# Scan of a bidirectional Mamba-2 branch: its decay matrices formed by TensorE in PSUM instead of by ScalarE, VectorE and GpSimd from broadcast rows

## The chip, the cores and the metric

The program runs on one core of a Trainium2 chip. The metric is the device time of one execution in microseconds (us), the median of several runs. The engines are named as the profile names them: PE is TensorE, DVE is VectorE, ACT is ScalarE, POOL is GpSimd and SP is SyncE, whose queue issues all the DMAs here.

## What is computed

The kernel is one layer of a diffusion backbone: a normalised input of 1024 tokens by 1024 channels feeds three branches (a bidirectional state-space scan, a Fourier mixing and a gated MLP), their outputs are gated and merged, and a feed-forward part with a short convolution follows. The change touches the scan alone. Its reference, cut to that part, for one direction:

```python
cum = jnp.cumsum(dt * a, axis=-1)                      # per chunk of 128 tokens, per head
lmat = jnp.exp(jnp.where(tri_q, cum[..., :, None] - cum[..., None, :], -jnp.inf))
cb = jnp.einsum('bcqgn,bcsgn->bcgqs', cf, bf)
y_diag = jnp.einsum('bcgqs,bgrcqs,bcsgrp->bcqgrp', cb, lmat, xf)   # xf = x * dt
y_off = jnp.einsum('bcqgn,bcgrpn,bgrcq->bcqgrp', cf, prev, jnp.exp(cum))
y = y_diag + y_off
```

The second direction runs over the flipped sequence with its own `dt` and `a`, and the two results are added. There are 16 heads of 64 channels in two groups of 8, and 8 chunks of 128 tokens. For each chunk and head a matrix of 128 by 128 factors is needed: the forward one below the diagonal plus the backward one above it, each exp of a difference of two running sums times a step size, times `cb`, which all heads of a group share.

## The kernel before, in words

The products with the big weight matrices run over all 1024 tokens. Each output tile of 128 channels is 48 products of 128 by 128 weights with 512 columns (`mm3`, L145 to L157: weights and inputs are split in a high and a low fp32r part, three products for each of 8 blocks and 2 halves). Its result lies in a PSUM tile of 1024 columns from the pool `psm` (tag `mm`, two buffers, `ps_big`, L48). The other four PSUM banks are single buffers with the tags `c`, `c2`, `t` and `y` (`ps_small`). PSUM is then full.

The scan of one group is `ssd_group`. It is called for group 0 after the context tokens' states are known (`ctx_state`), and for group 1 after `group_in(1)`, which computes group 1's inputs: tiles 9 and 11 (the `B` and `C` of the scan), x tiles 4 to 7, and, as filler between them, the tiles of the Fourier branch (`f_tile`, `psf0` to `psf3`). Behind the second scan stand the tiles `psz0` to `psz3`, `psu0` to `psu3` and `psv0`, `psv1`. A scheduler orders the instructions of each engine at build time, by priority and by what its own model takes to be free; it may put products of a later big tile between those of the scan, as far as their PSUM buffer is free. The engines then run their queues strictly in that order.

In one chunk `c` of `ssd_group` the steps are these. `y_off` (L511 to L519) runs once for the forward and once for the backward direction: two DMAs broadcast a chunk's running sums from DRAM into a tile `ro` (`decay_rows`, tag `ro` with two buffers, of which each direction in effect has one), ACT takes exp of it (L504), PE forms `po` from the state `st` (L514), DVE multiplies the two (L517) and POOL or DVE adds the result to `yacc` (L519). `state_step` (L521 to L531) carries the state on: POOL scales X and the old state, PE forms `pS` (L527), DVE adds (L531). Between them, for two half groups of four heads (`hg`): two DMAs of 256 KB broadcast the running sums of both directions (`rload`, L495: tiles `rf` and `rs`). For each head ACT subtracts the column's sum (L561), DVE subtracts the other direction's and takes the smaller of the two (L562), ACT and DVE form from the two masked copies of `cb` a matrix `G` of step sizes times `cb` (L564, L565). ACT takes exp of four heads at once (L567), POOL multiplies with `G` (L568), PE multiplies with X into `py` (L573), and DVE adds `py` to `yacc` (L576).

The lines that steer this:

```python
psm = pool("psm", bufs=2, space=bass.MemoryType.PSUM)
...
def ps_big(name):
    return psm.tile([P, 1024], F32, tag="mm", name=name)
...
r = s3.tile([P, 4, P], F32, tag="ro", name=f"ro{d_}{g}{c}")
```

Of the kernel before, what the change touches and what calls it, by code (L numbers as in the profile page):

```python
# [32 lines left out]
def hybrid_block_kernel(ctx: ExitStack, tc: tile.TileContext, a, dbg=None):  # L33
# [18 lines left out]
    def ps_small(name, tag="c"):  # L52
        return pss.tile([P, 512], F32, tag=tag, name=name)
# [6 lines left out]
    def bc(ap, shape):  # L60
        return ap.broadcast_to(shape)
# [430 lines left out]
    def rload(c, d_, g, hg, nm, tag):  # L492
        r = s3.tile([P, 4, P], F32, tag=tag, name=f"{nm}{g}{c}{hg}")
        o = d_ * 16 + g * 8 + hg * 4
        SY.dma_start(r, Rd[c, o:o + 4, :].partition_broadcast(P))  # L495
        return r
# [37 lines left out]
    def xload(g, c, nm):  # L534
        X = s3.tile([P, 512], F32, tag="X" + nm, name=f"X{nm}{g}{c}", bufs=2 if nm == "f" else 1)
        SY.dma_start(X, Xd[g][c])
        return X

    def ssd_group(g, BT, Bt, CT):
# [6 lines left out]
        scr[1, g] = s3.tile([P, L], F32, tag="scr", name=f"scr1{g}", bufs=1)  # L546
        for c in range(NCH):
            X = xload(g, c, "f")
            pcb = ps_small(f"pcb{g}{c}", "c")
            PE.matmul(pcb[:, 0:P], BT[:, c * P:(c + 1) * P], CT[:, c * P:(c + 1) * P], start=True, stop=True)  # L550
            cbm = s3.tile([P, 2, P], F32, tag="cbm", name=f"cbm{g}{c}", bufs=1)
            V.tensor_tensor(cbm, bc(pcb[:, 0:P].unsqueeze(1), [P, 2, P]), msk, op=ALU.mult)  # L552
            y_off(g, c, 0, stf, CT, G)
            py = ps_small(f"py{g}{c}", "y")
            for hg in range(2):
                E = rload(c, 0, g, hg, "rf", "rf")
                rs = rload(c, 1, g, hg, "rs", "rs")
                Gm = s3.tile([P, 4, P], F32, tag="G", name=f"G{g}{c}{hg}")
                for h in range(4):
                    f = g * 8 + hg * 4 + h  # L560
                    S.activation(E[:, h, :], E[:, h, :], AF.Identity, bias=ncum[:, c, f:f + 1])  # L561
                    V.scalar_tensor_tensor(E[:, h, :], rs[:, h, :], ncum[:, c, 16 + f:17 + f], E[:, h, :],  # L562
                                           op0=ALU.add, op1=ALU.min)
                    S.activation(Gm[:, h, :], cbm[:, 0, :], AF.Copy, scale=dtl[:, c, f:f + 1])  # L564
                    V.scalar_tensor_tensor(Gm[:, h, :], cbm[:, 1, :], dtl[:, c, 16 + f:17 + f], Gm[:, h, :],  # L565
                                           op0=ALU.mult, op1=ALU.add)
                S.activation(E, E, AF.Exp)  # L567
                G.tensor_tensor(E, E, Gm, op=ALU.mult)  # L568
                for h in range(4):
                    hd = (4 * hg + h) * 64  # L570
                    j = h % 2
                    i = 2 * hg + h // 2
                    PE.matmul(py[64 * j:64 * j + 64, i * P:(i + 1) * P], X[:, hd:hd + 64], E[:, h, :],  # L573
                              start=True, stop=True)
# [24 lines left out]
    Rd = dram.tile([NCH, 32, P], F32, name="Rd")  # L599
    psr = ps_small("psr")  # L600
    for i in range(2):
        PE.transpose(out=psr[:, i * P:(i + 1) * P], in_=cums[:, 4 * i:4 * i + 4, :].rearrange("p c h -> p (c h)"),
                     identity=ident)
    Rs_ = ddp.tile([P, 2, P], F32, tag="ul", name="Rs_")
    S.activation(Rs_, psr[:, 0:2 * P].rearrange("p (i q) -> p i q", i=2), AF.Copy)
    SY.dma_start(Rd.rearrange("(i c) h q -> (c h) i q", i=2), Rs_)
    yacc[0] = mpool.tile([P, 4, L], F32, tag="m", name="yacc0")
# [10 lines left out]
    s3 = pool("s3", bufs=2, side="right")  # L618
    ssd_group(0, *gi)
# [1064 lines left out]
def prepare(i):  # L1684
# [9 lines left out]
    r["tabc"], r["tabl"] = tabc, tabl  # L1694
    wm = i["w_mod"][0]
# [49 lines left out]
```

## Time and profile before

| what | value |
|---|---|
| runs shown (three) | 1888.46, 1881.87, 1887.11 us; median 1887.11 |
| the profiled execution | 1883.76 us, its span 1882.0 us |
| PE busy / weight loads | 1747.4 us (93%) / 1409.2 us (75%) |
| DVE, ACT, POOL busy | 1383.9 us (74%), 859.9 us (46%), 856.0 us (45%) |
| granted TensorE clock, mean | 0.967 |
| DMA | 268.75 MB, mean 143 GB/s |

The span is the part of the execution in which the engines ran instructions; 1.8 us lie around it. Busy shares count the time between an instruction's start and its (for PE modelled) end, so that a PE shown as busy may still stream fewer columns than it could: its records overlap. Where a stage is to be judged, the start of one product to the start of the next tells more than the busy share.

### The profile page before, as it was taken

How to read it: one execution, taken by the hardware profiler on the slowest of the kernel's cores; microseconds unless marked ns; L12 is line 12 of the kernel's file. 1: busy time of each engine (PE TensorE's matmuls, PEld its weight loads, DVE VectorE, ACT ScalarE, POOL GpSimd, SP SyncE). 2: the span in 40 equal slices, each digit the busy share in tenths (PEclk: the TensorE clock that was granted, in tenths of full speed). 3: DMA queues.
4: the chain of work that ended last, by engine and by line, in shares of the span. 5: the costliest groups of instructions: out<-in, count | busy, mean ns of one | idle time of the engine just before them, and what ended most of it. 6: DMA issues, size and time to landing. Idle time of an engine off the chain costs nothing. (4 is left out here: it accounts for less than half of the span.)

```text
span 1882.0 us, 23647 instructions
## 1 busy us (share of the span) xinstructions
PE 1747.4 (93%) x8148; PEld 1409.2 (75%) x8148; DVE 1383.9 (74%) x1983; ACT 859.9 (46%) x1480; POOL 856.0 (45%) x579
## 2 busy tenths in 40 slices
PE   4899998988989989999899999799999999899988
PEld 2688776766668868888688888578888888677777
DVE  7875577777573675557949536998888889967896
ACT  6644355564442344444524234445555455533433
POOL 3322355556531464554645745633333333544553
PEclk9999999999999989999998999899999999999998
DMA  9211365553454225765346464122232225553532
GB/s 336 101 59 61 118 191 159 154 159 116 148 183 160 107 85 184 235 224 184 118 146 201 129 230 140 40 90 96 95 126 104 96 96 174 199 187 106 174 111 90
DMA packets 148064, 268.75 MB, mean 143 GB/s; under 512 B 15836, under 2 KB 56668, under 8 KB 146536
## 3 DMA queue, kind: packets, MB, share of 16 engines
q1 hardware_dynamic: 147944, 267.25, 43.0%
q8 instruction: 64, 1.05, 0.2%
q14 instruction: 56, 0.46, 0.1%
HBM read 209.90 MB, written 57.29 MB: 142 GB/s over the span
## 5 line engine op out<-in xcount | busy, mean ns | idle before, releaser
L293 DVE SCALAR_TENSOR_TENSOR acc<-psx,convw,acc 128x1023 f32<-128x1023 f32 (+1 forms) x48 | 61.3, 1277 | 22.5 <-ACT acc L289 22.1
L562 DVE SCALAR_TENSOR_TENSOR rf<-rs,ncuml,rf 128x128 f32<-128x128 f32 x128 | 52.2, 454 | 32.4 <-ACT rf L561 29.2
L1272 POOL TENSOR_TENSOR pwo<-rwo,pwo 128x512 fp32r<-128x512 f32 x32 | 46.8, 1467 | 48.5 <-ACT pwo L1271 43.4
L857 POOL TENSOR_TENSOR w1up<-A11up,w1up 128x512 fp32r<-128x512 f32 x20 | 26.8, 1342 | 89.8 <-ACT w1up L856 80.6
L568 POOL TENSOR_TENSOR rf<-rf,G 128x512 f32<-128x512 f32 x32 | 46.1, 1442 | 43.1 <-DVE G L565 33.0
L857 POOL TENSOR_TENSOR w7up<-S3up,w7up 128x512 fp32r<-128x512 f32 x20 | 28.8, 1438 | 77.5 <-ACT w7up L856 45.0
L565 DVE SCALAR_TENSOR_TENSOR G<-cbm,dtl,G 128x128 f32<-128x128 f32 x128 | 57.0, 504 | 5.1 <-ACT G L564 5.1
L1561 DVE SCALAR_TENSOR_TENSOR xf<-Yd,g,xf 128x512 f32<-128x512 f32 x64 | 47.1, 743 | 13.0 <-PE Yd L867 12.7
L561 ACT ACTIVATE rf<-rf,ncuml 128x128 f32<-128x128 f32 x128 | 41.1, 389 | 29.5 <-DMA rf<-Rd 29.3
L166 ACT ACTIVATE gh<-gr 128x1024 fp32r<-128x1024 f32 (+1 forms) x36 | 37.1, 1034 | 38.0 <-DMA gr<-Gd 37.1
L157 PE MATMUL pso<-mh,pwo 128*128 128x512 f32 x128 | 50.2, 392 | 0.0
L153 PE MATMUL pso<-mh,pwo 128*128 128x512 f32 x128 | 49.8, 390 | 0.0
L155 PE MATMUL pso<-ml,pwo 128*128 128x512 f32 x128 | 49.8, 389 | 0.0
L517 DVE TENSOR_TENSOR scr<-po,ro 128x512 f32<-128x512 f32 x32 | 21.8, 683 | 35.2 <-ACT ro L504 35.0
L527 PE MATMUL pS<-scr,Bt 128*128 128x512 f32 x56 | 32.9, 671 | 15.4 <-DVE scr L517 12.0
L504 ACT ACTIVATE ro<-ro 128x512 f32<-128x512 f32 x32 | 20.1, 627 | 57.4 <-DMA ro<-Rd 57.1
L564 ACT ACTIVATE G<-cbm,dtl 128x128 f32<-128x128 f32 x128 | 39.6, 388 | 7.4 <-DVE cbm L552 7.4
L167 DVE TENSOR_TENSOR gl<-gr,gh 128x1024 fp32r<-128x1024 f32 (+1 forms) x26 | 39.7, 1527 | 4.2 <-ACT gh L166 3.6
L1477 DVE TENSOR_TENSOR gt<-gt,aa 128x512 f32<-128x512 f32 x44 | 42.5, 967 | 0.1
L1474 ACT ACTIVATE ft<-aa 128x512 f32<-128x512 f32 x44 | 27.8, 631 | 30.0 <-DVE aa L1456 29.0
L529 POOL TENSOR_TENSOR st<-st,etl 128x512 f32<-128x512 f32 x24 | 26.5, 1106 | 31.6 <-DVE st L531 31.6
L857 POOL TENSOR_TENSOR w4up<-A22up,w4up 128x512 fp32r<-128x512 f32 x20 | 30.9, 1544 | 21.4 <-ACT w4up L856 21.4
(1291 smaller groups left out, 6622.6 us busy)
## 6 DMA issues: line engine op xcount, KB each, us to landing
gr<-Gd SPq DMA_DIRECT2D x70, 256.0 KB, 3.7
Gd<-gt SPq DMA_DIRECT2D x10, 1536.0 KB, 5.7
wm<-in_wmod_dram SPq DMA_DIRECT2D x16, 512.0 KB, 9.6
ro<-Rd SPq DMA_DIRECT2D x64, 128.0 KB, 3.3
rf<-Rd SPq DMA_DIRECT2D x32, 256.0 KB, 4.3
rs<-Rd SPq DMA_DIRECT2D x32, 256.0 KB, 3.8
ctanh<-in_wmod_dram SPq DMA_DIRECT2D x32, 256.0 KB, 4.3
crow<-in_wmod_dram SPq DMA_DIRECT2D x32, 256.0 KB, 4.4
```

Of the source, the lines that this page charges most:

```text
L153: PE.matmul(o, wh[:, k, :], xh[:, sl], start=st, stop=False)
L155: PE.matmul(o, wh[:, k, :], xl[:, sl], start=False, stop=False)
L157: last_op["mm"] = PE.matmul(o, wl[:, k, :], xh[:, sl], start=False, stop=sp)
L293: V.scalar_tensor_tensor(acc[:, lo:hi], ps[:, lo + o:hi + o], cw[:, t, j:j + 1], acc[:, lo:hi], op0=ALU.mult, op1=ALU.add)
L561: S.activation(E[:, h, :], E[:, h, :], AF.Identity, bias=ncum[:, c, f:f + 1])
L562: V.scalar_tensor_tensor(E[:, h, :], rs[:, h, :], ncum[:, c, 16 + f:17 + f], E[:, h, :], op0=ALU.add, op1=ALU.min)
L565: V.scalar_tensor_tensor(Gm[:, h, :], cbm[:, 1, :], dtl[:, c, 16 + f:17 + f], Gm[:, h, :], op0=ALU.mult, op1=ALU.add)
L568: G.tensor_tensor(E, E, Gm, op=ALU.mult)
L857: (V if p in on_v else G).tensor_tensor(t[:, 1, :], ap, f32(t)[:, 0, :], op=ALU.subtract)
L1272: G.tensor_tensor(t[:, 1, :], raw, f32(t)[:, 0, :], op=ALU.subtract)
L1477: V.tensor_tensor(gt[:, 2 * q + h, :], gt[:, 2 * q + h, :], aa[:, HS[h]], op=ALU.mult)
L1561: V.scalar_tensor_tensor(xv, src, g2[:, dd:dd + 1], xv, op0=ALU.mult, op1=ALU.add)
```

## The change

Per chunk, half group and direction, the exponents of four heads come from TensorE. Each running sum is split into two fp32r parts, high and low, and written to DRAM as rows (`Rr[0]`); a second set of rows holds the logarithm of the step size less the running sum (`Rr[1]`, from a Ln on ACT, which brings two loads of activation tables). Before a scan, `Lt` is filled with ones and with the rows of the second set; for each chunk and direction two rows of the first set are loaded into `Rt`, under 16 rows of zeros and ones. A product of 18 rows, `Lt` with `Rt`, gives the 128 by 512 exponents, and a second product of the identity with `neg` adds -1e30 where the mask excludes (L498, L499). Both directions' exponents stand in one PSUM tile `E` of `ps_big`, the pool of the big tiles. ACT takes exp of each half (L575, L576), DVE adds the halves (L577) and multiplies with `cb` (L579), which ACT has copied out of PSUM (L566); PE multiplies with X as before (now L584). `rload`, the small ACT and DVE steps per head and POOL's multiplication are gone. The lines of the other steps move: `ro`'s load and exp to L507 and L508, `po` to L518, `scr` to L521, `yacc` to L523 and L587, the scaled X to L528, `pS` to L531, the state to L533 and L535.

```diff
--- before.py
+++ after.py
@@ -489,11 +489,15 @@
             filler()
         return BT, Bt, CT
 
-    def rload(c, d_, g, hg, nm, tag):
-        r = s3.tile([P, 4, P], F32, tag=tag, name=f"{nm}{g}{c}{hg}")
-        o = d_ * 16 + g * 8 + hg * 4
-        SY.dma_start(r, Rd[c, o:o + 4, :].partition_broadcast(P))
-        return r
+    def quad(c, d_):
+        return 32 * (2 * (c % 2) + d_)
+
+    def exponents(E, c, d_, hg, Lt):
+        q = quad(c, d_)
+        o = E[:, 512 * d_:512 * d_ + 512]
+        PE.matmul(o, Lt[q:q + 18, c // 2, :], Rt[q:q + 18, 512 * hg:512 * hg + 512], start=True, stop=False)
+        PE.matmul(o.rearrange("p (h q) -> p h q", h=4), identr, bc(neg[:, d_].unsqueeze(1), [P, 4, P]),
+                  start=False, stop=True)
 
     def decay_rows(c, d_, g):
         r = s3.tile([P, 4, P], F32, tag="ro", name=f"ro{d_}{g}{c}")
@@ -544,33 +548,40 @@
         stf, stb = st0
         scr[0, g] = tpool.tile([P, L], F32, tag="zz", name=f"scr0{g}", bufs=1)
         scr[1, g] = s3.tile([P, L], F32, tag="scr", name=f"scr1{g}", bufs=1)
+        Lt = s3.tile([P, 4, P], F32R, tag="Lt", name=f"Lt{g}", bufs=1)
+        S.activation(Lt, bc(ones.unsqueeze(1), [P, 4, P]), AF.Copy)
+        for c in range(2):
+            for d_ in range(2):
+                for l_ in range(2):
+                    q, o = quad(c, d_) + 8 * l_, d_ * 16 + g * 8
+                    SY.dma_start(f32(Lt)[q:q + 8], Rr[1][l_, c::2, o:o + 8, :].rearrange("c h q -> h c q"))
         for c in range(NCH):
             X = xload(g, c, "f")
+            for d_ in range(2):
+                q, o = quad(c, d_), d_ * 16 + g * 8
+                SY.dma_start(f32(Rt)[q + 16:q + 18], Rr[0][:, c, o:o + 8, :].rearrange("l h q -> l (h q)"))
             pcb = ps_small(f"pcb{g}{c}", "c")
             PE.matmul(pcb[:, 0:P], BT[:, c * P:(c + 1) * P], CT[:, c * P:(c + 1) * P], start=True, stop=True)
-            cbm = s3.tile([P, 2, P], F32, tag="cbm", name=f"cbm{g}{c}", bufs=1)
-            V.tensor_tensor(cbm, bc(pcb[:, 0:P].unsqueeze(1), [P, 2, P]), msk, op=ALU.mult)
+            cb = s3.tile([P, P], F32, tag="cb", name=f"cb{g}{c}")
+            S.activation(cb, pcb[:, 0:P], AF.Copy)
             y_off(g, c, 0, stf, CT, G)
             py = ps_small(f"py{g}{c}", "y")
             for hg in range(2):
-                E = rload(c, 0, g, hg, "rf", "rf")
-                rs = rload(c, 1, g, hg, "rs", "rs")
-                Gm = s3.tile([P, 4, P], F32, tag="G", name=f"G{g}{c}{hg}")
-                for h in range(4):
-                    f = g * 8 + hg * 4 + h
-                    S.activation(E[:, h, :], E[:, h, :], AF.Identity, bias=ncum[:, c, f:f + 1])
-                    V.scalar_tensor_tensor(E[:, h, :], rs[:, h, :], ncum[:, c, 16 + f:17 + f], E[:, h, :],
-                                           op0=ALU.add, op1=ALU.min)
-                    S.activation(Gm[:, h, :], cbm[:, 0, :], AF.Copy, scale=dtl[:, c, f:f + 1])
-                    V.scalar_tensor_tensor(Gm[:, h, :], cbm[:, 1, :], dtl[:, c, 16 + f:17 + f], Gm[:, h, :],
-                                           op0=ALU.mult, op1=ALU.add)
-                S.activation(E, E, AF.Exp)
-                G.tensor_tensor(E, E, Gm, op=ALU.mult)
+                E = ps_big(f"E{g}{c}{hg}")
+                for d_ in range(2):
+                    exponents(E, c, d_, hg, Lt)
+                ef = s3.tile([P, 512], F32, tag="ef", name=f"ef{g}{c}{hg}")
+                eb = E[:, 512:1024]
+                S.activation(ef, E[:, 0:512], AF.Exp)
+                S.activation(eb, eb, AF.Exp)
+                V.tensor_tensor(eb, ef, eb, op=ALU.add)
+                w_ = s3.tile([P, 4, P], F32, tag="G", name=f"G{g}{c}{hg}")
+                V.tensor_tensor(w_, eb.rearrange("p (h q) -> p h q", h=4), bc(cb.unsqueeze(1), [P, 4, P]), op=ALU.mult)
                 for h in range(4):
                     hd = (4 * hg + h) * 64
                     j = h % 2
                     i = 2 * hg + h // 2
-                    PE.matmul(py[64 * j:64 * j + 64, i * P:(i + 1) * P], X[:, hd:hd + 64], E[:, h, :],
+                    PE.matmul(py[64 * j:64 * j + 64, i * P:(i + 1) * P], X[:, hd:hd + 64], w_[:, h, :],
                               start=True, stop=True)
             yv = y_view(g, c)
             V.tensor_tensor(yv, py.rearrange("p (i q) -> p i q", i=4), yv, op=ALU.add)
@@ -597,13 +608,27 @@
     xbc_post(10, psb10, CT)
     n2w, nfw, ssdd, ssdn, fcw, fcb = late_consts()
     Rd = dram.tile([NCH, 32, P], F32, name="Rd")
+    Rr = [dram.tile([2, NCH, 32, P], F32, name=f"Rr{i}") for i in range(2)]
     psr = ps_small("psr")
-    for i in range(2):
-        PE.transpose(out=psr[:, i * P:(i + 1) * P], in_=cums[:, 4 * i:4 * i + 4, :].rearrange("p c h -> p (c h)"),
+    lds = ddp.tile([P, NCH, 32], F32, name="lds", tag="w" + "l")
+    V.tensor_scalar(lds, dtl, 1e-37, None, op0=ALU.max)
+    S.activation(lds, lds, AF.Ln)
+    V.tensor_tensor(lds, lds, cums, op=ALU.subtract)
+    for i in range(4):
+        PE.transpose(out=psr[:, i * P:(i + 1) * P],
+                     in_=(cums, lds)[i // 2][:, 4 * (i % 2):4 * (i % 2) + 4, :].rearrange("p c h -> p (c h)"),
                      identity=ident)
+    pr4 = psr.rearrange("p (i q) -> p i q", i=4)
     Rs_ = ddp.tile([P, 2, P], F32, tag="ul", name="Rs_")
-    S.activation(Rs_, psr[:, 0:2 * P].rearrange("p (i q) -> p i q", i=2), AF.Copy)
+    S.activation(Rs_, pr4[:, 0:2], AF.Copy)
     SY.dma_start(Rd.rearrange("(i c) h q -> (c h) i q", i=2), Rs_)
+    for j in range(2):
+        rh = ddp.tile([P, 2, P], F32R, tag=("rl", "t2l")[j], name=f"rh{j}")
+        rl = ddp.tile([P, 2, P], F32R, tag=("ql", "lal")[j], name=f"rl{j}")
+        S.activation(rh, pr4[:, 2 * j:2 * j + 2], AF.Copy)
+        V.tensor_tensor(rl, pr4[:, 2 * j:2 * j + 2], f32(rh), op=ALU.subtract)
+        for q, t in enumerate((rh, rl)):
+            SY.dma_start(Rr[j][q].rearrange("(i c) h q -> (c h) i q", i=2), f32(t))
     yacc[0] = mpool.tile([P, 4, L], F32, tag="m", name="yacc0")
     for i, ts in enumerate(((9,), (4, 5), (6,), (7,))):
         x_tile(0, i, True)
@@ -616,6 +641,14 @@
     s3 = pool("s3", bufs=2, side="right")
+    neg = s3.tile([P, 2, P], F32R, name="neg", bufs=1)
+    V.tensor_scalar(neg, msk, -1.0, 1e30, op0=ALU.add, op1=ALU.mult)
+    identr = s3.tile([P, P], F32R, name="identr", bufs=1)
+    S.activation(identr, ident, AF.Copy)
+    Rt = s3.tile([P, L], F32R, name="Rt", bufs=1)
+    ind = s3.tile([P, L], F32, tag="scr", name="ind", bufs=1)
+    SY.dma_start(ind, a["ind"])
+    S.activation(Rt, ind, AF.Copy)
     ssd_group(0, *gi)
     with tc.issue_after(last_op["state"].ins):
         V.tensor_scalar(fcw[:, 0:NFF, :], fcw[:, 0:NFF, :], 0.5, None, op0=ALU.mult)
...
```

How the order of the queues moves is shown at three places.

PE, scan of group 0, the third chunk, before (`po` and `pS` of the states, `py` of the outputs; `psx5` is a big tile, x tile 5 of group 1):

```order
L514 MATMUL po104_2046<-CT0_592,st105_1960 128x128 x4
L445 MATMUL pstx40_2768<-cst_95,acc4_2757 128x128 x4
L157 MATMUL psx5_2845<-hh0_289,wx5l_2841 128x512
L153 MATMUL psx5_2845<-hh1_326,wx5h_2840 128x512 x2
L155 MATMUL psx5_2845<-hl1_327,wx5h_2840 128x512 x2
L157 MATMUL psx5_2845<-hh1_326,wx5l_2841 128x512 x2
L153 MATMUL psx5_2845<-hh2_363,wx5h_2840 128x512 x2
L155 MATMUL psx5_2845<-hl2_364,wx5h_2840 128x512 x2
L157 MATMUL psx5_2845<-hh2_363,wx5l_2841 128x512 x2
L153 MATMUL psx5_2845<-hh3_400,wx5h_2840 128x512 x2
L527 MATMUL pS002_1939<-scr00_1667,Bt0_591 128x512
L155 MATMUL psx5_2845<-hl3_401,wx5h_2840 128x512 x2
```

Now, the same part of the scan one chunk on (`E040` and `E041` are the exponents of the two half groups of chunk 4):

```order
L584 MATMUL py03_1954<-G030_1964,Xf03_1935 64x128 x4
L498 MATMUL E040_2031<-Rt_1687,Lt0_1697 128x512
L499 MATMUL E040_2031<-neg_1683,identr_1685 128x512
L498 MATMUL E040_2031<-Rt_1687,Lt0_1697 128x512
L499 MATMUL E040_2031<-neg_1683,identr_1685 128x512
L518 MATMUL po103_2072<-CT0_592,st104_2008 128x128 x4
L584 MATMUL py03_1954<-G031_1979,Xf03_1935 64x128 x4
L498 MATMUL E041_2046<-Rt_1687,Lt0_1697 128x512
L499 MATMUL E041_2046<-neg_1683,identr_1685 128x512
L498 MATMUL E041_2046<-Rt_1687,Lt0_1697 128x512
L499 MATMUL E041_2046<-neg_1683,identr_1685 128x512
L531 MATMUL pS003_1987<-scr00_1695,Bt0_591 128x512
```

Before, the products of `psx5` stand between those of the scan; now only products of the scan follow each other. From the first product of the scan of group 0 to the last but one chunk's end no product of a big tile stands on PE's queue, and the same holds for group 1 from the last x tile on.

PE, the end of the scan of group 0 now (`psx9` is the first tile of `group_in(1)`):

```order
L531 MATMUL pS006_2215<-scr00_1695,Bt0_591 128x512
L564 MATMUL pcb07_2243<-CT0_592,BT0_590 128x128
L518 MATMUL po007_2251<-CT0_592,st006_2217 128x128 x4
L584 MATMUL py07_2258<-G070_2268,Xf07_2239 64x128 x4
L153 MATMUL psx9_2313<-hh0_289,wx9h_2308 128x512 x2
L155 MATMUL psx9_2313<-hl0_290,wx9h_2308 128x512 x2
L157 MATMUL psx9_2313<-hh0_289,wx9l_2309 128x512 x2
```

`psx9`, `psf0`, `psx11` and `psf1`, which stood ahead of or inside the scan of group 0, now follow it, as do x tiles 4 to 7 with `psf2` and `psf3`; `psz0` and all that comes behind it follow the scan of group 1.

ACT, scan of group 0, around the row tile `ro` of chunk 4, before:

```order
L504 ACTIVATE ro104_2042<-ro104_2042 128x512
L504 ACTIVATE ro004_2067<-ro004_2067 128x512
L561 ACTIVATE rf030_1981<-rf030_1981,ncuml_747 128x128 x4
L447 ACTIVATE xt4_2767<-pstx41_2774 128x512
L561 ACTIVATE rf031_2008<-rf031_2008,ncuml_747 128x128 x4
L567 ACTIVATE rf030_1981<-rf030_1981 128x512
L564 ACTIVATE G030_1985<-cbm03_1967,dtl_738 128x128 x4
```

Now:

```order
L508 ACTIVATE ro004_2019<-ro004_2019 128x512
L575 ACTIVATE ef040_2036<-E040_2031 128x512
L576 ACTIVATE E040_2031<-E040_2031 128x512
L575 ACTIVATE ef041_2051<-E041_2046 128x512
L508 ACTIVATE ro103_2068<-ro103_2068 128x512
L576 ACTIVATE E041_2046<-E041_2046 128x512
```

The exp of `ro` still stands ahead of a chunk's other work on ACT, which is now the two exps of each half group.

DVE, the same place, now (from the multiplication with chunk 3's forward `ro` to that with chunk 4's):

```order
L521 TENSOR_TENSOR scr00_1695<-po003_1947,ro003_1943 128x512
L577 TENSOR_TENSOR E040_2031<-ef040_2036,E040_2031 128x512
L587 TENSOR_TENSOR yacc0_892<-py03_1954,yacc0_892 128x4x128
L535 TENSOR_TENSOR st003_1989<-st003_1989,pS003_1987 128x512
L521 TENSOR_TENSOR scr10_1696<-po103_2072,ro103_2068 128x512
L577 TENSOR_TENSOR E041_2046<-ef041_2051,E041_2046 128x512
L523 TENSOR_TENSOR yacc0_892<-yacc0_892,scr10_1696 128x4x128
L579 TENSOR_TENSOR G040_2040<-E040_2031,cb04_2017 128x512
L579 TENSOR_TENSOR G041_2055<-E041_2046,cb04_2017 128x512
L535 TENSOR_TENSOR st103_2084<-st103_2084,pS103_2082 128x512
L521 TENSOR_TENSOR scr00_1695<-po004_2023,ro004_2019 128x512
```

Ten steps separate the two multiplications with `ro003` and `ro004`, and the first of them is the addition that follows chunk 4's first exps; in the scan of group 1 both additions of a chunk stand ahead, and five steps separate the second addition's start from the end of the multiplication with `ro`.

## Rows read from the trace of the kernel before

**Rows 1.** Stage from 236 to 558 us: PE, PEld, DVE, ACT, POOL busy, clock, DMA, GB/s.

```profile
236.00:558.00 322.00, 287.83 (x1455) 216.64 (x1454) 229.20 (x415) 170.84 (x380) 174.82 (x126) 0.96 0.52 154
```

**Rows 2.** Timeline of PE, stage's ends: start us, us, operation, count.

```profile
190.12 0.63 PE L153 MATMUL psx<-hh,wx9h 128*128 128x512 f32 x2
...
557.41 0.61 PE L157 MATMUL psv<-hh,wv1l 128*128 128x512 f32 x2
```

**Rows 3.** Timeline of PE, neighbours in scan 0 and one later.

```profile
261.56 1.10 PE L527 MATMUL pS<-scr,Bt 128*128 128x512 f32 x2
262.50 1.05 PE L514 MATMUL po<-CT,st 128*128 128x128 f32 x8
263.31 0.48 PE L155 MATMUL psx<-hl,wx4h 128*128 128x512 f32 x1
...
278.07 0.62 PE L153 MATMUL psf<-hh,wf2h 128*128 128x512 f32 x2
278.52 0.62 PE L155 MATMUL psf<-hl,wf2h 128*128 128x512 f32 x2
...
553.10 0.66 PE L573 MATMUL py<-rf,Xf 128*64 128x128 f32 x8
```

**Rows 4.** Groups by line, 190 to 558 us: busy us, mean ns, idle before.

```profile
L565 DVE SCALAR_TENSOR_TENSOR G<-cbm,dtl,G 128x128 f32<-128x128 f32 x128 | 57.0, 504 | 5.1 <-ACT G L564 5.1
L562 DVE SCALAR_TENSOR_TENSOR rf<-rs,ncuml,rf 128x128 f32<-128x128 f32 x128 | 52.2, 454 | 32.4 <-ACT rf L561 29.2 <-DMA rs<-Rd 2.9
L568 POOL TENSOR_TENSOR rf<-rf,G 128x512 f32<-128x512 f32 x32 | 46.1, 1442 | 43.1 <-DVE G L565 33.0 <-PE psx L157 6.2 <-DVE rf L562 3.1
L561 ACT ACTIVATE rf<-rf,ncuml 128x128 f32<-128x128 f32 x128 | 41.1, 389 | 29.5 <-DMA rf<-Rd 29.3
L564 ACT ACTIVATE G<-cbm,dtl 128x128 f32<-128x128 f32 x128 | 39.6, 388 | 7.4 <-DVE cbm L552 7.4
...
L517 DVE TENSOR_TENSOR scr<-po,ro 128x512 f32<-128x512 f32 x32 | 21.8, 683 | 35.2 <-ACT ro L504 35.0 <-issue 0.2
...
L504 ACT ACTIVATE ro<-ro 128x512 f32<-128x512 f32 x32 | 20.1, 627 | 57.4 <-DMA ro<-Rd 57.1 <-ACT rf L561 0.3
```

**Rows 5.** Waits from 190 to 558 us: total us, times, longest us.

```profile
ACT ro L504 <- DMA ro<-Rd: 57.1, 21, 6.3
DVE scr L517 <- ACT ro L504: 35.0, 11, 6.8
```

**Rows 6.** DMAs: L503's issues (ns), their landing (us); median landings of Xd and Xb.

```profile
L503 SPq DMA_DIRECT2D ro<-Rd x64: 573/580/1037, 231.3 to 533.1; - x64
...
DMA to landing us min/median/max: 2.9/3.3/7.8
...
Xb<-Xd SPq DMA_DIRECT2D x14, 256.0 KB, 3.3
Xd<-xt SPq DMA_DIRECT2D x4, 512.0 KB, 3.5
```

**Rows 7.** Timeline of DVE, the context tokens' last steps and states.

```profile
195.59 1.36 DVE L298 SCALAR_TENSOR_TENSOR cacc<-ctmp,cacc 128x256 f32<-128x256 f32 x2 [0.23 <-ACT ctmp L297]
...
208.18 1.28 DVE L403 TENSOR_TENSOR ctxm<-ctxm,wdc 128x512 f32<-128x512 f32 x2
...
232.26 0.69 DVE L410 TENSOR_TENSOR ctxm<-ctxm,pS 128x512 f32<-128x512 f32 x1 [1.33 <-PE pS L406]
```

**Rows 8.** Groups by line, 190 to 558 us: the steps behind an x tile.

```profile
L293 DVE SCALAR_TENSOR_TENSOR acc<-psx,convw,acc 128x1022 f32<-128x1022 f32 (+1 forms) x25 | 31.9, 1278 | 6.2 <-ACT acc L289 5.9
...
L297 ACT ACTIVATE tmp<-acc 128x1024 f32<-128x1024 f32 x7 | 7.4, 1052 | 6.3 <-DVE acc L293 4.0 <-DMA Xd<-xt 2.4
```

**Rows 9.** Timeline of PE and stage 404 to 411 us: a wait and the clock behind it.

```profile
404.90 2.08 PE L527 MATMUL pS<-scr,Bt 128*128 128x512 f32 x2 [3.44 <-POOL scr L524]
...
404.00:411.00 7.00, 6.10 (x10) 3.52 (x11) 6.96 (x5) 2.06 (x4) 7.00 (x5) 0.51 0.62 144
```

**Rows 10.** One line's instructions: the load of an activation table (ns).

```profile
L1187 ACT ACT_TABLE_LOAD  x1: 1283/1283/1283, 681.1 to 681.1; - x1
```

More of the change, by code (lines that the diff above doesn't have):

```diff
@@ L1694, in prepare @@
     r["tabc"], r["tabl"] = tabc, tabl
+    ind = np.zeros((4, 32, 8, P), np.float32)
+    for h in range(8):
+        ind[:, [h, h + 8], h] = 1.0
+    r["ind"] = ind.reshape(P, L)
     wm = i["w_mod"][0]
```

## The prediction

> **What bounds the kernel now.** I read the busy shares by stage first, then the timeline of PE, the groups by line, and the waits. From 236 to 558 us PE is the busiest engine: 287.8 of 322 us at a granted clock of 0.96, while DVE has 229, POOL 175 and ACT 171 [rows 1]. The reader should see that no other engine is near its own limit. So in this stage a step on ACT, DVE or POOL costs time only where PE has nothing to put in its place. The stage that the change can move runs from the first product of `psx9`, 190.1 us, to the last of `psv1`, 558.0 us [rows 2]: 368 us. Ahead of it and behind it the same work stands in the same order.
>
> How much of the 368 us is PE's own work? A 128x512 product of the big tiles takes 0.227 us from start to start (two in 0.45 us: 278.07 to 278.52), `pS` 0.94 and `po` 0.81, and `py` about 0.66 [rows 3]. Twenty big tiles of 48 products are 218 us. One chunk of the scan is 2 x 0.94 + 2 x 0.81 + 0.66 + 0.1 = 4.3 us, sixteen are 68; transposes and context states add some 15. About 301 us in all, so some 67 us are lost in 368. PE's waits in the scan stay that small because a big tile's product nearly always stands next on its queue. I keep this apart from a second thing: the scan by itself is slow. ACT waited 57.1 us for `ro`'s DMA, up to 6.3 at a time, and DVE 35.0 us for ACT's exp of it [rows 5].
>
> **What is taken away.** DVE loses 57.0 + 52.2 us, POOL 46.1, ACT 41.1 + 39.6 [rows 4], and one pair of row loads per half group goes. I cost all of it at nothing gained by itself: PE's products cover it now, and where the cover goes (below), another chain is longer than it.
>
> **What is added.** Eight products per chunk, 8 x 0.227 = 1.8 us: PE's chunk becomes 6.1 us, 29 us over both groups. No row shows a product of 18 rows, or one with a repeated mask as its input. The bounds are 0.227 us (both operands have the type of the big tiles, which I take) and `pS`'s 0.94, by which a chunk takes 11.8 us. On ACT each half group gets two exps; the nearest row is 0.627 us for 128x512 [rows 4]. On DVE it gets an add and a multiplication, one with two operands in PSUM; the nearest is `scr`, one operand in PSUM, 0.683. Bounds: 0.64 (half of a 1024-wide step, 1.28 [rows 8]) to 0.8 (my allowance for the second operand and the PSUM output). The Ln brings two table loads of 1.28 us [rows 10], near the context tokens' preparation, long before 190 us; ACT has slack there, and its price without that cover is 2.6 us. Rows in DRAM, transposes and small copies stand there too, at nothing; uncovered, at most about 4 us.
>
> **What is moved, and decides.** `E` takes the PSUM buffers of the big tiles, in program order. With two buffers, a later tile can't be started before the scan has had its last `E`. On PE's queue the scan of group 0 now has only its own products; ten tiles follow it (`psx9`, `psf0`, `psx11`, `psf1`, then x tiles 4 to 7 with `psf2` and `psf3`), and ten follow the scan of group 1. So the two scans no longer hide behind 218 us of products. They stand in line with them, and the scan's own longest loop becomes the price.
>
> That loop is the row tile. Each direction has in effect one buffer for `ro`: the multiplication with it must end before SP issues the next two DMAs; these land, ACT takes exp, and then DVE must come to the next multiplication. On ACT that exp stands ahead of the next chunk's exps of `E`, on DVE the add that needs those stands ahead of the rest. So ACT's wait for the DMA holds back everything behind it, and the steps add up. From rows: hand-over 0.06, issue 0.58, landing 3.3 after it [rows 6], `ro`'s exp 0.63, two exps of 0.62, then in the scan of group 0 ten DVE steps of 0.68: 12.6 us per chunk. In the scan of group 1 five DVE steps stand there: 9.2 us. PE's 6.1 us fits in either, and so do ACT's (6 x 0.63 + 0.4 = 4.2) and POOL's work. Queued behind `ro`'s waiting DMA on SP are only loads of later chunks.
>
> **The sum**, against the profiled execution (span 1882.0, total 1883.8 us):
> - Context tokens: the last convolution step ends at 195.59 + 1.36 = 197.0; 16 DVE steps of about 0.66 and some 1 us of waits [rows 7] bring the states to 208.6. Before, they ended at 233, spread out by the tiles between them.
> - About 12 issues on SP, 5 us; landing 3.3, exp 0.63, `scr` 0.68: first multiplication ends at 218.3.
> - Seven loops, four of 12.6 and three (first two, last) of about 11 where fewer steps stand between: 83.4. That is 301.7, and PE starts `psx9` near 301.
> - Ten tiles of 10.9, 40 transposes of 0.1, first products of the next scan, 2: 416.
> - Behind x tile 7 only a few products of the scan remain on PE, so its tail lies bare: ACT and DVE steps on it, 1.2 + 4 x 1.28 + 1.05 + 1.2 = 8.6 [rows 8], transposes and copies 2, the write `Xd` 3.5 and the read `Xb` or its forward twin 3.3 [rows 6], issue, `py` and its add 1.7: 19, so 435.
> - Seven loops of 9.2: 499.5; PE comes to `psz0` 3.5 us before that, 496; ten tiles and 1.5: 607.
>
> That is 607 - 558 = **49 us more**. The clock adds to it. Behind a wait of 3.44 us `pS` took 2.08 us in place of 1.10 [rows 9, 3], and 404 to 411 us ran at 0.51, the lower level. In the bare scans PE waits 3 to 6 us in each chunk, so its products will often run at that level; off the loop this costs nothing, but each return to dense tiles starts slow. A stretch like that of rows 9 loses 3.4 us; half of it at each of the two returns and a little in the loops gives 4. So 53 us, 1937 for the profiled execution. It lies 3.4 us under the median of the runs shown; I forecast **1938 us**. Steps of 0.64 to 0.8 move this by -5 to +14, a landing of 2.9 in place of 3.3 by -6, one of 4 by +10, bare covers by +6: with these not all on one side, the likeliest case's own range is 1915 to 1958.
>
> **The rivals.**
> - *Half clock through both scans.* PE's chunk takes 12.2 us, level with 12.6 in group 0 but 3.0 over 9.2 in group 1: 21 us there and, as DVE's steps then wait for `po` and `pS` at places in group 0, some 9: 1968. For: rows 9. Against: PE needs only every second microsecond. The slower bound of the added products ends near it: 11.8 - 9.2 = 2.6 over seven chunks, 18 us: 1956. Chance 0.2. In the Trainium skill, "TensorE: Matmul & The Clock Gate", section "A second HAM failure mode: psum-queue depth-cycling", short idle times between groups of products make the clock oscillate and cost throughput; by that this rival's 1968 would be likelier than my 1938. Rows 9 agree on the direction, no row here shows a whole scan like it.
> - *The row loop doesn't bind.* If `ro` is fetched far enough ahead, DVE's ten steps per chunk, 6.8 to 7.2 us, bind instead: 7 x 5 = 35 less in group 0, 7 x 2.1 = 15 less in group 1: 1888, no change. For: DVE is then nearly dense. Against: one buffer per direction, and the 57.1 us of rows 5 with the same buffers. Chance 0.1.
> - *Faster: big tiles still fill PE.* If one of the two PSUM buffers stayed with the big tiles during the scan, the 67 us lost could go for 29 us of products: about 38 less, 1846 to 1851. It decides from about five tile products per chunk between those of the scan. Against: the order of PE's queue has none. Chance 0.03.
>
> **How the numbers follow.** My forecast has 0.67, half clock 0.2, the unbound loop 0.1, faster 0.03. The range reaches from 1900, between unbound loop and forecast, to 1970, just past half clock; some 0.1 is left out on each side. The median can be told from no change beyond 0.5%, 9.4 us. Faster takes 0.03; no change takes most of the unbound loop, 0.07; slower the rest, 0.90.
>
> **What would show it.** In the changed kernel's timeline PE should have no product of a big tile between `po` of the first chunk and that of the last; `psx9` should start near 301 and `psz0` near 496, `psv1` end near 607; ACT's exp of `ro` (L508) should wait for its DMA at nearly every chunk, and starts of `scr` (L521) of one direction lie 12.6 and 9.2 us apart; the clock should fall below 0.9 in the scan's slices. DVE, ACT and POOL should have some 66, 55 and 46 us less (for DVE 109 off and 64 x 0.68 on, for ACT 81 off, 32 x 0.63 and 16 copies of 0.4 on). I am wrong if a chunk's period is about 7 us, if PE shows big tiles inside the scan, or if PE's products in the scan of group 1 leave no idle time.

## The result, and the profile after

The changed kernel takes 1945.38 us (median of four runs, 1936.70 to 1947.73), the kernel before 1887.78 (four runs): 1.0302 times as long, 95% interval 1.0266 to 1.0338. It is slower by 57.6 us; 1938 was forecast, in a range of 1900 to 1970. The profiled execution took 1936.70 us, 52.9 more than the profiled one of before, where the sum gave 53.

So the total came out. The terms that it was added up from did not, as the stages show. Stages of the changed kernel (from:to, length, then busy us and instructions of PE, PEld, DVE, ACT, POOL, then PE's clock, the DMA share, GB/s):

```profile
190.00:618.70 428.70, 394.01 (x1809) 283.07 (x1809) 195.60 (x251) 137.04 (x198) 139.98 (x102) 0.94 0.33 103
...
190.00:223.00 33.00, 17.85 (x62) 10.00 (x61) 19.45 (x31) 9.79 (x16) 8.20 (x5) 0.84 0.42 132
...
413.00:437.00 24.00, 13.61 (x36) 6.84 (x38) 11.80 (x12) 11.06 (x16) 3.63 (x3) 0.62 0.31 93
...
228.00:296.00 68.00, 63.25 (x332) 36.96 (x332) 48.37 (x79) 28.59 (x54) 36.11 (x34) 0.98 0.40 115
445.00:503.00 58.00, 55.80 (x280) 32.45 (x281) 42.04 (x61) 22.41 (x42) 27.70 (x26) 0.94 0.36 106
```

The same stage of the kernel before, to the end of the same tile (`psv1`):

```profile
190.00:558.00 368.00, 333.58 (x1651) 251.35 (x1650) 255.92 (x449) 186.44 (x400) 189.38 (x134) 0.97 0.50 149
```

The stage grew by 60.7 us (some 3 us of the work ahead of it and behind it lie inside it now, and about 6 come back later). DVE lost 60, ACT 49 and POOL 49 us there, near the forecast 66, 55 and 46. PE stood idle for 428.7 - 394.0 = 34.7 us, where it had stood idle for 368.0 - 333.6 = 34.4 before: **no more idle time, but 60 us more of busy time.** The idle time only moved: 25 us of it now lie ahead of the two scans (190 to 223 us and 413 to 437 us). In the bare scans themselves PE is busy for 63 of 68 and 56 of 58 us. The forecast had it waiting for half of the time in group 0 and for a third in group 1.

Why PE is full there stands in its timeline, one chunk of the scan of group 1 in the changed kernel (start, length, then in brackets idle time before and its releaser):

```profile
482.56 2.05 PE L518 MATMUL po<-CT,st 128*128 128x128 f32 x16 [0.37 <-ACT cb L566]
484.55 0.66 PE L584 MATMUL py<-G,Xf 128*64 128x128 f32 x8
485.13 0.50 PE L498 MATMUL E<-Rt,Lt 18*128 18x512 f32 x1
485.56 0.50 PE L499 MATMUL E<-neg,identr 128*128 128x512 f32 x1
485.99 0.50 PE L498 MATMUL E<-Rt,Lt 18*128 18x512 f32 x1
486.42 0.49 PE L499 MATMUL E<-neg,identr 128*128 128x512 f32 x1
486.84 0.66 PE L584 MATMUL py<-G,Xf 128*64 128x128 f32 x8
...
489.05 1.88 PE L531 MATMUL pS<-scr,Bt 128*128 128x512 f32 x4
490.85 0.49 PE L564 MATMUL pcb<-CT,BT 128*128 128x128 f32 x2
491.70 1.49 PE L518 MATMUL po<-CT,st 128*128 128x128 f32 x11 [0.37 <-ACT cb L566]
```

From `po` to `po` it is 9.14 us, and PE waits for 0.37 of them (this is one of the four chunks at the full clock; two more took 10.6 us, partly at the lower level). The added products start 0.43 us after each other, not 0.227: 128 x 0.43 = 55 us, nearly the whole loss. The prediction had that price as a bound (between 0.227 and 0.94) and took the low end. Between the weight loads of such products PE's load queue stands idle for about 0.24 us:

```profile
487.43 0.18 PEld L498 LDWEIGHTS E<-Rt,Lt 18*128 18x128 f32 x1 [0.17 <-issue]
487.85 0.19 PEld L499 LDWEIGHTS E<-neg,identr 128*128 128x128 f32 x1 [0.25 <-issue]
488.28 0.18 PEld L498 LDWEIGHTS E<-Rt,Lt 18*128 18x128 f32 x1 [0.24 <-issue]
```

The steps on ACT and DVE cost what their neighbours did [rows 4], two PSUM operands or not, and the row tile's waits became shorter than in [rows 5]. Groups by line, 190 to 613 us of the changed kernel (busy us, mean ns, idle before and what ended it):

```profile
L577 DVE TENSOR_TENSOR E<-ef,E 128x512 f32<-128x512 f32 x32 | 22.1, 689 | 11.5 <-ACT E L576 11.5
L579 DVE TENSOR_TENSOR G<-E,cb 128x512 f32<-128x512 f32 x32 | 20.9, 682 | 0.8 <-ACT cb L566 0.7
L575 ACT ACTIVATE ef<-E 128x512 f32<-128x512 f32 x32 | 19.0, 594 | 42.6 <-PE E L499 42.2
```

Its waits in the same stretch (us, times, longest):

```profile
ACT ro L508 <- DMA ro<-Rd: 24.9, 16, 5.7
DVE scr L521 <- ACT ro L508: 12.3, 4, 9.9
```

Two theories went into the experiments. **A**, the prediction's: the scans stand bare on PE, so their own chains are the price. **B**: the price is PE's work on the added products, wherever they stand. Two more came up on the way, on why such a product takes 0.43 us. **C**: it is the change between products of 18 and of 128 rows. **D**: it is the mask product itself, with its repeated input, or the accumulation into one bank.

### The profile page after: what moved, and what is told of

The parts are those of the page before. It is cut to its first block, busy times and chain, and to the rows that moved or that the text cites. A ratio compares the mean times of both kernels' runs of the same rounds, so it can differ in the third digit from the quotient of the medians.

```text
span 1934.9 us, 23480 instructions
## 1 busy us (share of the span) xinstructions
PE 1804.5 (93%) x8278; PEld 1437.3 (74%) x8278; DVE 1313.3 (68%) x1780; ACT 812.0 (42%) x1281; POOL 808.7 (42%) x547
## 5 line engine op out<-in xcount | busy, mean ns | idle before, releaser
L521 DVE TENSOR_TENSOR scr<-po,ro 128x512 f32<-128x512 f32 x32 | 21.9, 686 | 29.4 <-PE po L518 16.8
L498 PE MATMUL E<-Rt,Lt 18*128 18x512 f32 x64 | 34.6, 540 | 5.9 <-DMA Rt<-Rr 3.1
L1508 DVE SCALAR_TENSOR_TENSOR aa<-ft,aa 128x512 f32<-128x512 f32 x44 | 37.9, 862 | 2.0 <-ACT ft L1507 1.9
L167 POOL TENSOR_TENSOR gl<-gr,gh 128x1024 fp32r<-128x1024 f32 x10 | 27.4, 2743 | 26.5 <-ACT gh L166 26.5
L898 PE MATMUL Yup<-bhh,w7up 128*128 128x512 f32 x80 | 32.1, 401 | 6.5 <-DVE Uup L1089 6.5
L890 POOL TENSOR_TENSOR w5up<-S1up,w5up 128x512 fp32r<-128x512 f32 x20 | 31.0, 1548 | 16.1 <-ACT w5up L889 16.0
L575 ACT ACTIVATE ef<-E 128x512 f32<-128x512 f32 x32 | 19.0, 594 | 42.6 <-PE E L499 42.2
L508 ACT ACTIVATE ro<-ro 128x512 f32<-128x512 f32 x32 | 20.1, 629 | 39.3 <-DMA ro<-Rd 24.9
L528 POOL TENSOR_TENSOR scr<-Xf,wdl 128x512 f32<-128x512 f32 x14 | 14.6, 1042 | 52.6 <-PE pS L531 35.6
```

Source lines behind the costliest of these rows:

```text
L167: return (lo_eng or G).tensor_tensor(lo, src, hi.bitcast(F32), op=ALU.subtract)
L498: PE.matmul(o, Lt[q:q + 18, c // 2, :], Rt[q:q + 18, 512 * hg:512 * hg + 512], start=True, stop=False)
L890: (V if p in on_v else G).tensor_tensor(t[:, 1, :], ap, f32(t)[:, 0, :], op=ALU.subtract)
L1508: V.scalar_tensor_tensor(ac, th, 1.0, ac, op0=ALU.add, op1=ALU.mult)
```

## The experiments

Ratios are to the kernel before, run on the same chip. The changed kernel stands at 1.0302.

### Exponents in a bank of their own, so that big tiles come back into the scan

```diff
-                E = ps_big(f"E{g}{c}{hg}")
                 for d_ in range(2):
+                    E = ps_small(f"E{d_}{g}{c}{hg}", "t")
                     exponents(E, c, d_, hg, Lt)
+                    S.activation(ew[d_], E, AF.Exp)
```

(The diff is cut to the lines that matter. `ew` holds two SBUF tiles, which DVE adds as before.)

> The exponents get a PSUM bank of their own (the 512-wide one of tag t, one direction after the other), so that big tiles keep their two buffers and their products stand between those of the scan again. Same products, same arithmetic. Theory A (the 53 us are lost because the scans stand bare on PE): most of it comes back, below 1905 us. Theory B (the 53 us are the 128 added products, 0.43 us each on an engine that is busy anyway; PE's idle time from 190 us on is 34 us before and 35 after): PE's work stays, 1920 to 1945 us.

Measured: 1936.43 us, ratio 1.0286 (1.0265 to 1.0307). The tiles do stand in the scan again, and the time is the same within the intervals. New in this run are two waits of PE (190 to 613 us):

```profile
PE psx L153 <- ACT fs L454: 11.0, 2, 5.9
```

Without them the time would be near 1925 us by my estimate, still far from the 1905 that A asked for. A alone falls. What the products cost can be seen between two products of a big tile (PE's timeline of this run):

```profile
288.79 0.39 PE L153 MATMUL psx<-hh,wx5h 128*128 128x512 f32 x1
289.10 0.50 PE L498 MATMUL E<-Rt,Lt 18*128 18x512 f32 x1
289.53 0.50 PE L499 MATMUL E<-neg,identr 128*128 128x512 f32 x1
289.87 0.39 PE L153 MATMUL psx<-hh,wx5h 128*128 128x512 f32 x1
290.10 0.39 PE L155 MATMUL psx<-hl,wx5h 128*128 128x512 f32 x1
```

Products of a big tile follow each other at 0.23 us; from the one before the pair to the one behind it is 1.08 us, where three such steps are 0.68.

### The kernel before, with its scans bare

```diff
-            py = ps_small(f"py{g}{c}", "y")
+            py = ps_big(f"py{g}{c}")[:, 0:512]
```

> The kernel before, with py taken from the big tiles' PSUM pool: its scans then stand bare on PE as in the changed kernel, with no product added. Theory A: the scan's own steps set the time, a chunk takes what DVE needs (8 x 0.50 + 8 x 0.45 + 4 x 0.68 + 0.4 = 10.8 us) or more against 4.3 us of PE work, so about 16 x 6.5 = 100 us are laid bare, less what the tiles before had lost (34): 1940 us or more. Theory B: no work is added to PE, so the time stays within 15 us of 1887.

Measured: 2002.55 us, 1.0640 (1.0622 to 1.0658): 121 us for the same arithmetic in the same amounts. B alone falls as well: what a bare scan costs depends on how long its steps on the other engines take for a chunk. The two scans in this run:

```profile
222.00:328.00 106.00, 59.98 (x272) 38.60 (x274) 96.58 (x171) 54.78 (x149) 59.78 (x50) 0.69 0.55 159
447.00:564.00 117.00, 65.70 (x293) 41.89 (x293) 90.31 (x163) 54.53 (x141) 58.34 (x48) 0.67 0.44 133
```

DVE is busy for 97 of 106 us, PE for 60, and the granted clock fell to 0.69 and 0.67, means of its two levels: here the prediction's half-clock rival is seen, at a PE that waits for some 45% of the time. In the Trainium skill, "TensorE: Matmul & The Clock Gate", section "A second HAM failure mode: psum-queue depth-cycling", short idle times between groups of products make the clock oscillate. These two rows agree; the changed kernel's scans, at 0.98 and 0.94 with PE nearly full, show where it does not come about. The run with 128 rows in the big tiles' buffers (below) does not agree: in its scan of group 1 PE waits 1.05 to 2.46 us ahead of `po` in every chunk after the first of the bare ones, at a granted clock of 1.00.

### The changed kernel without the mask product

```diff
-        PE.matmul(o.rearrange("p (h q) -> p h q", h=4), identr, bc(neg[:, d_].unsqueeze(1), [P, 4, P]),
-                  start=False, stop=True)
```

(The first product then ends the accumulation. In two lines that are not shown, exp is taken of the exponents times 1e-6, so that it stays finite without the mask.)

> The changed kernel without the second product (the mask is left out, and exp is taken of the exponents times 1e-6 so that it stays finite). 64 products fewer. Theory A with the row loop of the prediction (12.6 and 9.2 us per chunk, PE hidden under it): within 5 us of the changed kernel. Theory B: 64 x 0.43 = 27 us less, about 1918 us.

Measured: 1928.45 us, 1.0240 (1.0208 to 1.0271): 12 us less than the changed kernel, between the two. The wait that grew:

```profile
ACT ro L506 <- DMA ro<-Rd: 45.9, 19, 6.2
```

24.9 us had it been. With less work on PE, ACT waits longer for the row tile's DMA. This points to a second limit of the bare scan, close under the first; two of the runs below try it.

### One buffer per direction for the row tile

```diff
-        r = s3.tile([P, 4, P], F32, tag="ro", name=f"ro{d_}{g}{c}")
+        r = s3.tile([P, 4, P], F32, tag=f"ro{d_}", name=f"ro{d_}{g}{c}", bufs=1)
```

> The changed kernel with one buffer for the row tile of each direction (a tag for each), which is what the prediction took the pool to give. If that was so, nothing changes. If the pool hands each of its two buffers to the tile that comes next, of either direction, the forced loop now binds in the scan of group 0: up to 12.6 us per chunk in place of 9.8, some 20 us more; nothing in group 1, where PE takes 9.1.

Measured: 1942.24 us, 1.0324 (1.0294 to 1.0354): no difference that can be told. In its profile (of the slowest of its runs, 1951 us) the sixteen multiplications of the scan of group 0 start from 230.5 to 306.5 us, 10.1 us per chunk; in the changed kernel from 226.9 to 295.8, 9.2 us. Even with one buffer per direction forced, a chunk does not take the 12.6 us of the prediction. It is no full test of that loop, because the scheduler also gave DVE a new order: at 262.8 and 271.8 us the multiplications of both directions stand next to each other.

### The mask left out where big tiles stand between

The same product taken away in the first experiment's kernel, with exp again of the exponents times 1e-6.

> As the run with a PSUM bank of its own for the exponents, without the mask product (the mask is left out, exp is taken of the exponents times 1e-6). The changed kernel without it gained 12 us where 27 were expected; its waits for the row tile's DMA rose from 24.9 to 45.9 us. If the row loop of about 8.5 us per chunk had taken over there, it can't here, where big tiles stand between: 64 x 0.35 = 22 us or more come off, below 1915 us. If the product is simply cheaper than thought, 12 us again, about 1925 us.

Measured: 1916.21 us, 1.0151 (1.0122 to 1.0179): 1.35% under the 1.0286 of its base, 25 us, where 22 or more were expected. Where big tiles stand between the scan's steps, less work on PE is less time.

### The four products regrouped

```diff
-                for d_ in range(2):
-                    exponents(E, c, d_, hg, Lt)
+                for step in range(2):
+                    for d_ in range(2):
+                        exponents(E, c, d_, hg, Lt, step)
```

(Step 0 issues the product of 18 rows, step 1 that of the mask.)

> The changed kernel with the four products of a half group regrouped: the two of 18 rows first, then the two of the mask. Same work. Theory C: one change of rows in place of three, the four take about 1.1 to 1.3 us in place of 1.72, PE's chunk in the scan of group 1 falls from 9.1 us to about 8.2, and the row loop of about 8.5 us takes over: 8 to 12 us less. Rival D: the mask products follow each other at 0.43 us as before, no change.

Measured: 1931.52 us, 1.0226 (1.0195 to 1.0256), 14 us less where 8 to 12 were expected. The four in this run (x2: two instructions):

```profile
482.47 0.50 PE L499 MATMUL E<-Rt,Lt 18*128 18x512 f32 x2
482.90 0.73 PE L501 MATMUL E<-neg,identr 128*128 128x512 f32 x2
483.56 0.66 PE L587 MATMUL py<-G,Xf 128*64 128x128 f32 x8
```

Two products of 18 rows now take 0.43 us together, the four 1.09 in place of 1.71. One half of rival D falls: the mask products, with the same repeated input, come at 0.33 us each with the change to `py` counted in. The other half, two products in a row into one bank, does not occur in this order; the next run has it.

### The first product with 128 rows

The indicator rows are shared, `Rt` holds the rows of all chunks' sums once per group, and one-hot rows in the weights (32 more rows of `Lt`, the rest meets zeros in `Rt`) pick those of a chunk. On the base of the first experiment (the edits to the loads and to the rows are not shown):

```diff
-        PE.matmul(o, Lt[q:q + 18, c // 2, :], Rt[q:q + 18, 512 * hg:512 * hg + 512], start=True, stop=False)
+        PE.matmul(o, Lt[:, d_, :], Rt[:, 512 * hg:512 * hg + 512], start=True, stop=False)
```

> As the run with a PSUM bank of its own for the exponents, but the first product has 128 rows: the indicator rows are shared, the rows of all chunks' running sums stand in Rt once per group, and one-hot rows of the weights pick a chunk's two. Same result, as many products. In that run a big tile's product, the 18-row product, the mask product and the next big tile's product start 0.31, 0.43 and 0.34 us after each other, 1.08 in all. Theory C (the price is the change between products of 18 and of 128 rows, where the weights can't be loaded beside the running product): with 128 rows throughout 3 x 0.227 = 0.68, so 64 x 0.40 = 26 us less, about 1911 us. Rival D (it is the repeated mask or the accumulation into one bank that takes 0.43): no change, about 1936 us.

Measured: 1906.07 us, 1.0098 (1.0065 to 1.0130): 35 us under its base, with as many products. In its timeline they now follow at the pace of their neighbours:

```profile
267.89 0.39 PE L155 MATMUL psf<-hl,wf2h 128*128 128x512 f32 x1
268.12 0.39 PE L497 MATMUL E<-Rt,Lt 128*128 128x512 f32 x1
268.35 0.39 PE L498 MATMUL E<-neg,identr 128*128 128x512 f32 x1
268.57 0.59 PE L530 MATMUL pS<-scr,Bt 128*128 128x512 f32 x1
```

0.23 us each, with the mask product right behind the first one in the same bank: D falls. That is theory C: what cost 0.43 was the change between products of 18 and of 128 rows. In the Trainium skill, "TensorEngine Tiling (Array Packing)", section "Key Properties", changing the tiling mode drains the engine. The rows agree, if a product of 18 rows counts as another mode, which no run here shows by itself: the changes around one such product cost 1.08 - 0.68 = 0.40 us between big tiles. About 9 us of the 35 go beyond the expected 26; which part the other loads have in that (three into `Lt` per chunk in place of two into `Rt`) was not tried.

### 128 rows in the big tiles' buffers

The same edit in the changed kernel itself.

> The changed kernel, its exponents in the big tiles' buffers as there (the scans bare on PE), with the first product of 128 rows as in the run that took 1906 us. It completes the square of pool and rows: 1.0302 and 1.0286 of the kernel before with 18 rows (shared, own), 1.0098 with 128 rows and a bank of its own. If PE's work alone set the time (theory B), the shared pool loses the same as the own one: about 1.012, 1910 us. If the bare scan has a floor of its own just under PE's 9.1 us per chunk (the chain by the row tile and its DMA, about 8.5 us, seen when the mask was left out), PE's chunk of 7.5 us stands idle against it and only some 10 to 15 us come off: 1.022 to 1.026, 1927 to 1935 us.

Measured: 1932.06 us, 1.0242 (1.0212 to 1.0272). The square is complete:

| | 18 rows | 128 rows |
|---|---|---|
| shared with the big tiles (scans bare) | 1.0302 | 1.0242 |
| bank of its own (tiles in the scan) | 1.0286 | 1.0098 |

Cheaper products gain 35 us with tiles in the scan and 11 in the bare one; tiles in the scan gain 27 us with cheap products and 3 with dear ones. Either loss hides the other. The two scans as stages of this run:

```profile
231.00:296.00 65.00, 55.52 (x337) 37.82 (x335) 48.13 (x79) 28.66 (x55) 36.03 (x33) 0.99 0.44 128
437.00:496.00 59.00, 49.46 (x305) 33.24 (x304) 45.28 (x66) 21.77 (x43) 32.20 (x31) 1.00 0.37 112
```

`po` of four chunks in PE's timeline:

```profile
448.67 2.05 PE L517 MATMUL po<-CT,st 128*128 128x128 f32 x16 [2.46 <-ACT cb L566]
...
475.85 2.05 PE L517 MATMUL po<-CT,st 128*128 128x128 f32 x16 [1.72 <-ACT cb L566]
...
484.50 2.05 PE L517 MATMUL po<-CT,st 128*128 128x128 f32 x16 [1.05 <-ACT cb L566]
...
493.42 2.05 PE L517 MATMUL po<-CT,st 128*128 128x128 f32 x16 [1.32 <-ACT cb L566]
```

ACT's timeline at the second of them:

```profile
473.36 0.63 ACT L507 ACTIVATE ro<-ro 128x512 f32<-128x512 f32 x1 [1.83 <-DMA ro<-Rd]
...
475.52 0.27 ACT L566 ACTIVATE cb<-pcb 128x128 f32<-128x128 f32 x1
```

And ACT's wait for the row tile in all, 190 to 610 us:

```profile
ACT ro L507 <- DMA ro<-Rd: 45.2, 24, 4.0
```

PE's idle time in the scans is back (9.5 us in each). A chunk of group 1 takes 8.65 to 9.33 us, 8.95 on average from 448.67 to 493.42, and ACT's copy of `cb`, on which `po` waits, stands behind ACT's wait for the row tile. That is the floor of the bare scan, 0.2 us per chunk under PE's 9.14. In group 0 the cheaper products gained nothing: `psx9` starts at 295.9 us here and at 296.0 in the changed kernel.

### Transposes through the big tiles' buffers

In the run of 1906 us PE waits twice, for 5 to 6 us up to 369 and to 389 us, for ACT's copy of a big tile, which stands behind copies of transposed tokens. The idea was that the transposes come late because exponents hold bank `t`. Here they use `ps_big`.

> As the run with products of 128 rows and a PSUM bank of its own for the exponents, but the transposes of group 1's tokens go through the big tiles' buffers, because the exponents now hold bank t to the scan's end: between 320 and 400 us PE had 62 of 80 us busy there, with two waits of 5 to 6 us behind a copy that waits for a transposed x tile's write. If that is the last bare place, some 12 us come off: about 1893 us, within 1% of the kernel before. PE still has the 128 products more (128 x 0.227 = 29 us) than the kernel before, so by theory B it stays at or above 1888 us.

Measured: 1925.83 us, 1.0214 (1.0185 to 1.0244), a miss: 20 us more where 12 less were expected. Now a transpose that waits for its tile blocks PE's queue, and products of the exponents wait for ACT (waits of PE, 190 to 610 us):

```profile
PE pstx L450 <- DVE acc L298: 9.0, 1, 9.0
PE E L502 <- ACT G L581: 6.3, 5, 2.5
```

No version beat the kernel before. The best is 1.0% slower, and it still has the 128 products more, 29 us at 0.227.

## Why the prediction was right, and where it was not

- **Direction and size: right.** Nothing that ACT, DVE and POOL lost came back as time against the kernel before (it is worth something once the scans are bare: with the old steps they cost 121 us); the queue order told that the scans would stand bare, and they do: no tile stands between 223 and 296 us.
- **"PE's chunk becomes 6.1 us": the mis-sized term.** It is 9.1. Half of the 3.0 us between them is the added products, 0.43 in place of 0.227 each (regrouped and 128-row runs): the low bound was taken because both operands have the type of the big tiles, and the nearest row in type was not the nearest in shape. The other half lay in the chunk itself. The sum has `py` once, but each of the two half groups has one (1.17 us in place of 0.66); `po` took 1.99 in place of 1.62, and `pcb` with the wait behind it 0.85 in place of 0.1.
- **The row loop of 12.6 us in group 0: wrong.** The scan of group 0 took 69 us from its first multiplication to its last, not 83; forced to one buffer per direction it took 76 in its slowest run. The step that fails is that each direction has one buffer. Four instructions of the changed kernel show it, named by the order of the queues: DVE's multiplication with a backward tile, SP's loads of the forward `ro004`, DVE's multiplication with the forward `ro003`, and ACT's exp of `ro004`.

```profile
253.11 0.69 DVE L521 TENSOR_TENSOR scr<-po,ro 128x512 f32<-128x512 f32 x1 [0.28 <-ACT ro L508]
253.83 1.24 SPq L507 DMA_DIRECT2D ro<-Rd  x2
256.95 0.68 DVE L521 TENSOR_TENSOR scr<-po,ro 128x512 f32<-128x512 f32 x1
257.54 0.63 ACT L508 ACTIVATE ro<-ro 128x512 f32<-128x512 f32 x1 [2.52 <-DMA ro<-Rd]
```

  The loads of `ro004` started 3.1 us before the multiplication with `ro003`: they took the buffer that the backward tile had freed. So their landing did not add up with the ten DVE steps that follow the multiplication with `ro003`, and from there to the multiplication with `ro004` (266.67 us) it was 9.7 us. The rival of the unbound row loop had its condition right here, but not its price: DVE's ten steps are 7 us. Which steps set the 9.7 is open; PE's work alone does not, since the scan of group 0 stayed as long when it fell (128-row run).
- **9.2 us in group 1: right in number, not in cause.** PE's own work, with its wait for `cb`, takes 9.14 us there, so the prediction's own sign of being wrong came true: PE's products leave next to no idle time. The row loop's floor lies just under it, 8.95 us as soon as PE's work falls.
- **Context tokens and first multiplication:** states at 216.8 us in place of 208.6, end of the first multiplication at 227.6 in place of 218.3. These 9 us and the shorter scan partly cancel: `psx9` at 296.0, forecast near 301. Then the tiles end at 412.9 (416 with the first products of the next scan), `psz0` starts at 503.4 (496), and `psv1` ends at 618.7, with 1.7 us of later work inside (607, without such work). From the tiles' end to `psz0` six loops followed and not seven, since the first chunk's multiplications stood at 376 us among the tiles; but the second chunk's came only at 444.3, where 435 was forecast for the first.
- **The sum to the tenth: luck.** The first multiplication came 9 us late, the scan of group 0 was 14 us shorter, the way from the tiles' end to `psz0` about 9 us longer, and 6 us came back behind the stage. That these errors leave 52.9 beside 53 was not foreseen by any step of the sum.
- **Clock:** 4 us were put on for it; what it cost was not taken apart. 413 to 437 us ran at 0.62. Two waits of PE lie in it, and the products behind the first already run at the lower level (0.79 us in place of 0.50):

```profile
419.26 0.79 PE L498 MATMUL E<-Rt,Lt 18*128 18x512 f32 x1 [2.75 <-DVE G L579]
...
436.61 1.98 PE L584 MATMUL py<-G,Xf 128*64 128x128 f32 x16 [6.89 <-DMA Xf<-Xd]
```

  The scans ran at 0.98 and 0.94, where under 0.9 was forecast. The rival of half clock through both scans did not come; its cheaper neighbour, the slower bound of the added products, did in part.
- **Table loads:** two, long before 190 us as said (ACT's timeline). What they cost was not taken apart; in all, some 1.6 us of the work that was done by 190 us before now lie behind it:

```profile
116.43 1.28 ACT L615 ACT_TABLE_LOAD   x1
...
122.44 1.28 ACT L341 ACT_TABLE_LOAD   x1
```

- **The faster rival** asked for tiles between the scan's steps. The first experiment gave it that, and the time did not move: 55 us of dear products had taken the room. With cheap products it is worth 27 us, and even then the added products are work on the engine that bounds the stage.

## What to carry to other kernels

Where one engine is full in a stage, work that is moved onto it from engines with slack is paid in full, however much it relieves them: count the instructions moved onto the bound first. Price a new product by its shape as well as its type; one with few rows between products of 128 rows can take twice the time of its neighbours (0.43 and 0.23 us here), and filling it with zero rows up to 128 took that away. Count how often each product stands in one turn of a loop: one `py` left out was half a microsecond per chunk. When two limits lie close together, as 9.14 and 8.95 us per chunk here, undoing one alone shows little: try each, and then both.

## What the hardware showed that was not expected

- Two products of 18 rows and 512 columns in a row (in neighbouring groups of 32 rows) took 0.43 us together, a single one between products of 128 rows 0.43 alone.
- PE's granted clock stayed at 0.99 and 1.00 in scans where PE was busy for 55.5 of 65 and 49.5 of 59 us, and fell to 0.69 and 0.67 where it was busy for 60 of 106 and 65.7 of 117.
- A DVE addition with one operand and the result in PSUM took 0.689 us, a multiplication 0.682: the same as `scr` with one operand there.
